# Loading the input of a last-axis product in two chunks

## The chip, the cores and the metric

The kernel runs on one core of a Trainium2 chip. The metric is the device time of one execution in microseconds (us). The trace of an execution covers less than that: its span is 8.4 us where the device time is 10.19 us.

Three engines matter here: SyncE (SP) issues the transfers, 16 DMA engines carry them out in pieces called packets, and VectorE (DVE) multiplies. For the load of the kernel before, the trace shows 128 data packets, 16 semaphore packets (9 ns each) and 16 semaphore records, from 3.42 to 3.99 us. Here a transfer counts as landed at the last of its 16 records; the first multiply starts 0.023 us after it.

Runs are labelled fast or slow. For a program on one core the label only says whether a run is within 1.5% of the fastest run of the same kernel in its session. One execution in each set is profiled.

## The reference

```python
batch, seq, dim = 32, 64, 64
x = np.random.randn(batch, seq, dim).astype(np.float32) * 0.1 + 1.0
np.prod(x, axis=-1)          # 2048 products of 64 numbers each
```

The input is 512 KB of fp32, the output 8 KB.

## The kernel before

The 2048 rows are laid out as 128 partitions with 16 rows each, so that a partition holds 16 x 64 = 1024 elements, 4 KB. One load brings all of it. A tree of six multiplies then halves the rows: 512 products per partition, then 256, 128, 64, 32 and 16.

```python
x_view = xf.rearrange("(p n) d -> p n d", p=P)       # P = 128, n = 16
out_view = of.rearrange("(p n) -> p n", p=P)
with tc.tile_pool(name="sbuf", bufs=1) as pool:
    xt = pool.tile([P, n, R], x.dtype, name="xt")    # R = 64
    nc.sync.dma_start(out=xt[:], in_=x_view)
    cur = xt; cur_len = R; lvl = 0
    while cur_len > 1:
        half = cur_len // 2
        nxt = pool.tile([P, n, half], x.dtype, name=f"lvl{lvl}")
        nc.vector.tensor_tensor(out=nxt[:], in0=cur[:, :, 0:half],
                                in1=cur[:, :, half : 2 * half], op=mult)
        # ... (a branch for odd lengths, not taken here)
        cur = nxt; cur_len = half; lvl += 1
    nc.sync.dma_start(out=out_view, in_=cur[:, :, 0])
```

## Time and profile before

| | us |
|---|---|
| median of 6 runs | 10.19 (10.13 to 10.23) |
| span of the trace | 8.4 |
| load: issue to landing | 0.72 to 3.99 |
| six multiplies: first start to issue of the store | 4.01 to 6.21 |
| store: issue to landing | 1.4 |

The chain of work that ended last, in order of time (start in us, length in us, what; "issue" lines cut). It is one line with no branches: load, then multiplies.

```profile
0.72 3.26 DMA xt<-in_x_dram
...
4.01 0.70 DVE lvl_60 L51
...
4.73 0.43 DVE lvl_62 L51
...
6.00 0.17 DVE lvl_70 L51
```

The groups of instructions of the same kernel: line, engine, operation, output and input, shapes, count, then busy us and mean ns of one, then the idle time before it and what ended it. VectorE (DVE) is idle for 4.0 us and is released by the load. Halving the elements does not halve the time: 691 ns at 512 elements, 424 at 256, 174 at 16.

```profile
L51 DVE TENSOR_TENSOR lvl_60<-xt 128x512 f32<-128x512 f32 x1 | 0.7, 691 | 4.0 <-DMA xt<-in_x_dram 4.0
L51 DVE TENSOR_TENSOR lvl_62<-lvl_60 128x256 f32<-128x256 f32 x1 | 0.4, 424 | 0.0
L51 DVE TENSOR_TENSOR lvl_64<-lvl_62 128x128 f32<-128x128 f32 x1 | 0.3, 291 | 0.0
L51 DVE TENSOR_TENSOR lvl_66<-lvl_64 128x64 f32<-128x64 f32 x1 | 0.2, 226 | 0.0
L51 DVE TENSOR_TENSOR lvl_68<-lvl_66 128x32 f32<-128x32 f32 x1 | 0.2, 193 | 0.0
L51 DVE TENSOR_TENSOR lvl_70<-lvl_68 128x16 f32<-128x16 f32 x1 | 0.2, 174 | 0.0
```

The DMA row of the page shows the span in 40 slices of 0.21 us, in GB/s. Data flow from the ninth slice, 1.0 us after the issue at 0.72 us, and start slower than they go on: 195 to 254 GB/s in the first three slices, up to 429 later.

```profile
GB/s 0 0 0 0 0 0 0 0 195 254 215 390 312 371 429 254 78 0 0 0 0 0 0 0 0 0 0 0 0 0 0 0 0 22 17 0 0 0 0 0
```

The packet records behind that row: 128 packets of 4 KB, which is eight for each of 16 engines, from 1.72 to 3.64 us, typically 159 ns each. The semaphores that report the landing come in between 3.42 and 3.99 us.

### The profile page before, as it was taken

The numbers are of one execution on the slowest core, as the hardware profiler recorded it, in microseconds if no ns is written. First come the engines' busy times: TensorE is split into PE (matmuls) and PEld (weight loads), VectorE is DVE, ScalarE is ACT, GpSimd is POOL, SyncE is SP. The second block draws the span as 40 slices with busy tenths as digits, with TensorE's granted clock in tenths as the row PEclk, the third lists the DMA queues.
The fourth block names the chain that finished last, engine by engine and source line by source line (L and its number), as shares of the span: only waits on it lengthen the run. The fifth ranks groups of instructions, "written<-read, shape, count | busy, mean of one in ns | idle before, by whom it ended". The sixth has DMA issues, their size and how long they took to land.

```text
span 8.4 us, 50 instructions
## 1 busy us (share of the span) xinstructions
DVE 2.0 (24%) x6; POOL 0.2 (2%) x4
## 2 busy tenths in 40 slices
DVE  0000000000000000000999898988840000000000
POOL 0900000000000000000000000000000000000000
DMA  0000000089797996200000000000000002200000
GB/s 0 0 0 0 0 0 0 0 195 254 215 390 312 371 429 254 78 0 0 0 0 0 0 0 0 0 0 0 0 0 0 0 0 22 17 0 0 0 0 0
DMA packets 289, 0.53 MB, mean 63 GB/s; under 512 B 161, under 2 KB 161, under 8 KB 289
## 3 DMA queue, kind: packets, MB, share of 16 engines
q1 hardware_dynamic: 288, 0.53, 19.8%
q14 instruction: 1, 0.00, 0.0%
HBM read 0.52 MB, written 0.01 MB: 63 GB/s over the span
## 4 chain that ended last, share of the span: by engine, by line
DMA 39%; DVE 24%; issue 2%
DMA xt<-in_x_dram 39%; DVE lvl_60 L51 8%; DVE lvl_62 L51 5%; DVE lvl_64 L51 4%; DVE lvl_66 L51 3%; DVE lvl_68 L51 2%; DVE lvl_70 L51 2%
## 5 line engine op out<-in xcount | busy, mean ns | idle before, releaser
L51 DVE TENSOR_TENSOR lvl_60<-xt 128x512 f32<-128x512 f32 x1 | 0.7, 691 | 4.0 <-DMA xt<-in_x_dram 4.0
L51 DVE TENSOR_TENSOR lvl_62<-lvl_60 128x256 f32<-128x256 f32 x1 | 0.4, 424 | 0.0
L51 DVE TENSOR_TENSOR lvl_64<-lvl_62 128x128 f32<-128x128 f32 x1 | 0.3, 291 | 0.0
L51 DVE TENSOR_TENSOR lvl_66<-lvl_64 128x64 f32<-128x64 f32 x1 | 0.2, 226 | 0.0
L51 DVE TENSOR_TENSOR lvl_68<-lvl_66 128x32 f32<-128x32 f32 x1 | 0.2, 193 | 0.0
L51 DVE TENSOR_TENSOR lvl_70<-lvl_68 128x16 f32<-128x16 f32 x1 | 0.2, 174 | 0.0
L85 POOL MEMSET const-float32-0.0<- 128x1 f32 x1 | 0.1, 98 | 0.2 <-issue 0.2
L85 POOL MEMSET const-bfloat16-1.0<- 128x1 bf16 x1 | 0.1, 101 | 0.0
L85 POOL MEMSET const-uint8-127<- 128x1 uint8 x1 | 0.1, 101 | 0.0
L85 POOL MEMSET const-float32-1.0<- 128x1 f32 x1 | 0.1, 98 | 0.0
## 6 DMA issues: line engine op xcount, KB each, us to landing
xt<-in_x_dram SPq DMA_DIRECT2D x1, 512.0 KB, 3.3
out_dram<-lvl_70 SPq DMA_DIRECT2D x1, 8.0 KB, 1.4
```

Source lines behind the costliest of these rows:

```text
L51: nc.vector.tensor_tensor(out=nxt[:], in0=cur[:, :, 0:half], in1=cur[:, :, half : 2 * half], op=mybir.AluOpType.mult,)
L85: nc = _bacc.Bacc("TRN2", target_bir_lowering=False, num_devices=1)
```

## The change

The intent is to load the input in two chunks of 8 rows per partition, and to do the first two levels of the tree on chunk 0 while chunk 1 is still on its way. Both chunks write into one tile `comb`, from which the last four levels run unsplit. The diff also adds branches for other shapes and axes, which this input does not take; they are cut here.

```diff
-        xt = pool.tile([P, n, R], x.dtype, name="xt")
-        nc.sync.dma_start(out=xt[:], in_=x_view)
-        ... six multiplies over all 16 rows
+NSPLIT = 2
+PER_CHUNK_LEVELS = 2
...
+                comb = pool.tile([P, nr, w_comb], x.dtype, name="comb", tag="comb")
+                for k in range(nsplit):
+                    kr0 = r0 + k * cr
+                    comb_k = comb[:, k * cr : (k + 1) * cr, :]
+                    xt = pool.tile([P, cr, R], x.dtype, name=f"xt{k}", tag=f"xt{k}")
+                    nc.sync.dma_start(out=xt[:], in_=x_view[:, kr0 : kr0 + cr, :])
...
+                    for lv in range(per_chunk_levels):
...
+                        _level(nc, cur, dst)       # dst is comb_k in the last of them
...
+                res = _prod_tree(nc, pool, comb[:], x.dtype, tag="lvl")
+                nc.sync.dma_start(out=out_view[:, r0:r1], in_=res[:, :, 0])
```

The multiplies become `c0l` and `comb` of chunk 0 (256 and 128 elements per partition), the same for chunk 1 (`c1l`, `comb`), and then 128, 64, 32 and 16 elements.

## The prediction

> **What bounds the kernel now.** The chain of waits is one serial line. The load of 512 KB is issued at 0.72 us and lands at 3.99 us (3.26 us, 39% of the 8.4 us span); only then does VectorE start (timeline: first multiply at 4.01 us, after 4.0 us idle). The six multiplies take 691, 424, 291, 226, 193 and 174 ns (groups of instructions), with about 34 ns between starts and ends, so the store is issued at 6.21 us. The store takes 1.4 us to land (DMA issues); then comes a closing part, and 1.8 us lie outside the span (10.19 against 8.4).
>
> The load itself: the packets in the trace start at about 1.72 to 2.04 us, 1.0 us after the issue, staggered over the 16 engines by about the length of the issuing instruction (367 ns). After slow first packets (up to 466 ns) an engine takes 159 ns per 4 KB packet, eight packets each; the last data packet ends at 3.60 us, the last semaphore at 3.99 us.
>
> **What the change does.** Two chunks of 8 rows per partition. One load becomes two of 256 KB from the same queue, with 2 KB runs instead of 4 KB. Levels 1 and 2 are done per chunk, (512, 256) elements becoming 2 x (256, 128); the other four multiplies are unchanged, as is the store. VectorE's total rises from 2.00 us to 2.00 - 691 - 424 + 2 x (424 + 291) ns = 2.31 us. [...]
>
> **Critical path.** The second issue starts about 0.40 us after the first, near 1.12 us; [...] chunk 0's eight half-size packets (estimate: 80 ns each plus the slow start, 0.9 us) keep each engine busy to about 2.6 to 2.9 us. So the stream should not pause, and chunk 0 lands near 3.1 us. Its two multiplies (424 + 291 + gaps, 0.78 us) end near 3.9 us, before chunk 1 lands. After chunk 1's landing remain 424 + 291 + 291 + 226 + 193 + 174 = 1599 ns instead of 1999: 0.40 us saved. Given back: twice as many packets. [...] with an extra semaphore packet (9 ns in the trace) per engine I estimate 0.03 to 0.1 us, so chunk 1 lands near 4.05 us. One more semaphore to wait for or clear in the closing part: 0 to 0.06 us.
>
> **Prediction.** 10.19 - 0.40 + 0.06 + 0.03 = 9.88 us, 3% faster; 8 in 10 between 9.74 and 10.04. Faster by over 2%: 0.76; within 2%: 0.21; slower by over 2%: 0.03.
>
> **What would show each step.** Two issues about 0.40 us apart; first load landing at 2.9 to 3.3 us, second at 3.95 to 4.2; VectorE idle between chunk 0's second multiply and chunk 1's first one, ended by the second load; from the last landing to the store's issue 1.80 us instead of 2.20; packets of 2 KB near 80 ns; the store at 1.4 us.
>
> **What would make it wrong.** The second load starting its data only about 1 us after the first's last descriptor[...]: chunk 1 lands at 4.2 us or later and the gain halves. Chunk 0 landing late, its slowest engine waiting behind chunk 1's packets, so that its multiplies hold chunk 1 up. A longer closing part from the added semaphore.

## The result, and the profile after

The changed kernel took 9.97 us (median of 10 runs, 9.89 to 10.18) against 10.22 us for the kernel before (20 runs, 10.13 to 10.29). The ratio is 0.973 with a 95% interval of 0.968 to 0.978. Ratios here are the mean time of one kernel's fast runs over that of the other's of the same rounds, so they are not quite the ratio of the medians.

Two things make this result less firm than its interval. The ten runs fall in two groups, 9.89 to 10.00 us and 10.07 to 10.18 us, and the second group is what the label calls slow and leaves out. With all ten counted, the ratio of the means is 10.01 / 10.22 = 0.980. And the same kernel was measured three times more, on three chips:

| run | chip | before, us | changed, us | ratio of fast runs | 95% interval |
|---|---|---|---|---|---|
| first result | not recorded | 10.22 | 9.97 | 0.973 | 0.968 to 0.978 |
| e1_after_again | 4 | 10.20 | 10.11 | 0.991 | 0.987 to 0.995 |
| e8_after_again2 | 13 | 10.15 | 9.82 | 0.966 | 0.961 to 0.970 |
| e9_after_again3 | 7 | 10.20 | 10.01 | 0.971 | 0.961 to 0.980 |

The medians of the kernel before stay within 0.07 us of each other; those of the changed kernel range over 0.29 us. The gain is clear of noise in each session but lies between 0.9% and 3.4%. The ratio of e9 rests on two of its six runs; with all six it is 0.981.

The first profile after fell in a slow run (10.27 us). These are lines of its chain; chunk 0 landed at 3.81 us, and chunk 0's load and multiplies are on the chain.

```profile
0.73 3.08 DMA xt_59<-in_x_dram
...
3.83 0.44 DVE c0l_61 L24
...
4.29 0.29 DVE comb L24
4.58 0.34 DVE c1l_66 L24
```

Two profiles of fast runs of the same kernel were taken later, e1 (10.13 us) and e8 (9.83 us), and they show two different limits. First e8, its timeline (start, length, engine, line, operation, output and input; in brackets the idle time before it and what ended it; where two loads are meant, x2):

```profile
0.73 0.85 SPq L134 DMA_DIRECT2D xt<-in_x_dram  x2
3.40 0.42 DVE L24 TENSOR_TENSOR c0l<-xt 128x256 f32<-128x256 f32 x1 [3.40 <-DMA xt<-in_x_dram]
3.86 0.29 DVE L24 TENSOR_TENSOR comb<-c0l 128x128 f32<-128x128 f32 x1
4.07 0.42 DVE L24 TENSOR_TENSOR c1l<-xt 128x256 f32<-128x256 f32 x1
4.52 0.29 DVE L24 TENSOR_TENSOR comb<-c1l 128x128 f32<-128x128 f32 x1
...
5.86 0.35 SPq L158 DMA_DIRECT2D out_dram<-lvll  x1
```

There is no idle time before `c1l`: VectorE never waits again after its first multiply. The chain of e8 says the same, as it runs through chunk 0's load and both its multiplies:

```profile
0.73 2.65 DMA xt<-in_x_dram
...
3.40 0.43 DVE c0l L24
...
3.86 0.29 DVE comb L24
4.15 0.35 DVE c1l L24
```

Now the same lines of e1, first the timeline, then the chain. VectorE is idle for 0.19 us before `c1l`, and the chain goes through the second load, issued at 1.16 us and landed at 4.34 us.

```profile
3.42 0.42 DVE L24 TENSOR_TENSOR c0l<-xt 128x256 f32<-128x256 f32 x1 [3.42 <-DMA xt<-in_x_dram]
3.88 0.29 DVE L24 TENSOR_TENSOR comb<-c0l 128x128 f32<-128x128 f32 x1
4.36 0.43 DVE L24 TENSOR_TENSOR c1l<-xt 128x256 f32<-128x256 f32 x1 [0.19 <-DMA xt<-in_x_dram]
...
6.16 0.35 SPq L158 DMA_DIRECT2D out_dram<-lvll  x1
```

```profile
1.11 0.05 issue
1.16 3.18 DMA xt<-in_x_dram
4.34 0.02 issue
4.36 0.44 DVE c1l L24
```

With the landings from the semaphore records of the traces, the change of time can be added up. All three are fast runs:

| us | before | e8 | e1 |
|---|---|---|---|
| chunk 0 lands | | 3.381 | 3.392 |
| last chunk lands | 3.986 | 3.983 | 4.336 |
| its first multiply starts | 4.009 | 4.071 | 4.359 |
| store issued | 6.207 | 5.858 | 6.155 |
| end of span less issue of store | 2.189 | 2.190 | 2.195 |
| store issued earlier than before by | | 0.349 | 0.052 |
| run time less than before's 10.19 by | | 0.36 | 0.06 |

In each kernel an undelayed first multiply starts 0.023 us after the landing. From there to the store the kernel before takes 6.207 - 4.009 = 2.198 us, e8 5.858 - 4.071 = 1.787 us and e1 1.796 us. So the shorter chain saves 0.41 us in e8 and 0.40 us in e1. In e8 nothing is lost at the landing (-0.003 us), but `c1l` starts 4.071 - 3.983 - 0.023 = 0.065 us late because VectorE is still at chunk 0. In e1 the landing is 0.350 us late and the hold-up is zero. The closing part did not change.

Three more profiles have the same loads and the same order of multiplies: the first one after and e9, both labelled slow, and e10, fast, with other addresses for its chunks. They show both losses at once. In them chunk 1 landed 0.58 to 0.61 us after chunk 0, as in e8 (0.60; in e1 it was 0.94), and `c1l` was held up by 0.087, 0.083 and 0.064 us; the last landing was 0.41, 0.10 and 0.13 us later than before's. One caution: the landing of a single load moves too. It came at 4.07 us in e12 and at 4.12 us in e2 (both labelled slow), so a difference of 0.1 us between two profiles is not yet the effect of the split.

The windows view shows the two late stretches of the load in these runs (stretch, us, DVE busy, POOL busy, clock, DMA share, GB/s). Before, then e8, then e1:

```profile
3.20:3.60 0.40, 0.00 (x0) 0.00 (x0) 1.00 0.34 133
3.60:4.00 0.40, 0.00 (x0) 0.00 (x0) 1.00 0.00 0
```

```profile
3.20:3.60 0.40, 0.20 (x1) 0.00 (x0) 1.00 0.38 138
3.60:4.00 0.40, 0.37 (x2) 0.00 (x0) 1.00 0.01 5
```

```profile
3.20:3.60 0.40, 0.18 (x1) 0.00 (x0) 1.00 0.39 143
3.60:4.00 0.40, 0.36 (x2) 0.00 (x0) 1.00 0.09 36
```

A DMA share of 0.09 of 16 engines is one to two engines. In e1 nearly all of the data have come by 3.6 us, as in the others, and one or two engines are still at work to 4.02 us. The landing, at 4.336 us, comes after the end of that work. By the packet records, the last seven packets of e1 follow each other from 3.46 to 4.02 us and take 81 to 84 ns each: they started late, they were not slow.

### The profile page after: what moved, and what is told of

It reads as the page before. It is cut to its first block, busy times and chain, and to the rows that moved or that the text cites. A ratio compares the mean times of both kernels' runs of the same rounds, so it can differ in the third digit from the quotient of the medians.

```text
span 8.5 us, 54 instructions
## 1 busy us (share of the span) xinstructions
DVE 2.2 (26%) x8; POOL 0.2 (2%) x4
## 4 chain that ended last, share of the span: by engine, by line
DMA 36%; DVE 27%; issue 3%
DMA xt_59<-in_x_dram 36%; DVE comb L24 7%; DVE c0l_61 L24 5%; DVE c1l_66 L24 4%; DVE lvll_69 L24 4%; DVE lvll_71 L24 3%; DVE lvll_73 L24 2%; DVE lvll_75 L24 2%
## 5 line engine op out<-in xcount | busy, mean ns | idle before, releaser
L24 DVE TENSOR_TENSOR comb<-c0l_61 128x128 f32<-128x128 f32 x1 | 0.3, 293 | 0.0
L24 DVE TENSOR_TENSOR comb<-c1l_66 128x128 f32<-128x128 f32 x1 | 0.3, 293 | 0.0
```

Source lines behind the costliest of these rows:

```text
L24: nc.vector.tensor_tensor(out=dst[:, :, 0:half], in0=src[:, :, 0:half], in1=src[:, :, half : 2 * half], op=MULT,)
```

## The experiments

Two theories stood against each other after the result. Theory S is the prediction: chunk 0's work is hidden, and the time hangs on chunk 1's landing. Theory H: chunk 0 lands so late that its multiplies hold chunk 1 up. Later runs ask why chunk 1 lands late at all. Twelve runs were made, of ten kernels (e1, e8 and e9 are the changed one), each in five rounds; all results were correct except where a wrong result was intended.

### e1: the changed kernel again

No edit.

> The changed kernel unaltered, to get a profile of a fast run (the first one fell in a slow run) and a second measure of the ratio. Theory H (hold-up): chunk 0 lands so late that its two multiplies (0.78 us with gaps) end after chunk 1 has landed; VectorE then never idles after its first multiply and the chain is chunk 0's landing + 2.46 us; chunk 0 lands at 3.4 to 3.6 us, chunk 1 at 3.95 to 4.2 us. Rival S (stream, as predicted): chunk 0 lands at 2.9 to 3.3 us, VectorE idles 0.1 us or more before chunk 1's first multiply, and the store is issued 1.80 us after chunk 1's landing. Both: ratio 0.965 to 0.98.

Measured: 10.11 us, ratio 0.991, outside the expected 0.965 to 0.98. The profile, shown above, is a mixture. VectorE idles, and the store follows chunk 1's landing by 1.82 us, as S has it. But chunk 0 landed at 3.39 us, just past the 2.9 to 3.3 us of S, and chunk 1 at 4.34 us, past both theories. Here the load's end is the limit.

### e2: one load, multiplies in chunks

```diff
-level over xt[:, 0:16]; level over the result
+for a, b in [(0, 8), (8, 16)]:
+    level(nc, half[:], xt[:, a:b, :])
+    level(nc, comb[:, a:b, :], half[:])
```

> One 512 KB load as before, but the multiplies as in the change (levels 1 and 2 in two chunks of rows). Measures the added VectorE work alone: 2.46 us from first multiply to store issue instead of 2.20, so before + 0.26 us (10.48, ratio 1.025). Both theories expect the same; if it is under 1.015 my costing of the small multiplies is wrong.

Measured: 10.27 us, ratio 1.0025 (0.998 to 1.007): my costing was wrong by its own rule. The build had put both 256-element multiplies ahead of both 128-element ones. The timeline shows why they cost so little. Two multiplies of 422 ns on average take 0.76 us together, and the first of the next pair starts at 4.83 us, before the pair ends at 4.91 us.

```profile
4.15 0.76 DVE L15 TENSOR_TENSOR c<-xt 128x256 f32<-128x256 f32 x2 [4.15 <-DMA xt<-in_x_dram]
4.83 0.49 DVE L15 TENSOR_TENSOR comb<-c 128x128 f32<-128x128 f32 x2
5.35 0.29 DVE L15 TENSOR_TENSOR t<-comb 128x128 f32<-128x128 f32 x1
```

A multiply that does not need the result of the one in front starts 342 ns after it (4.149 and 4.491 us) instead of the 458 ns (3.404 and 3.862 us in e8) of a multiply that waits for a 256-element one. First multiply to store is 6.365 - 4.149 = 2.216 us, against 2.198 us before. (This profile is of a slow run; these durations agree with those of fast runs.) The changed kernel has the order chunk 0, chunk 0, chunk 1, chunk 1, and so has one such overlap, `c1l` over `comb`: 4.071 - 3.862 = 209 ns after it, where a waiting one needs 325. Its first multiply to store is 2.454 us.

So in both profiles a multiply that waits for no result starts some 0.12 us earlier than one that waits: 458 - 342 = 116 ns in e2, 325 - 209 = 116 ns in e8.

### e3: two loads, multiplies uncut

```diff
-nc.sync.dma_start(out=xt[:], in_=x_view)
+for a, b in [(0, 8), (8, 16)]:
+    nc.sync.dma_start(out=xt[:, a:b, :], in_=x_view[:, a:b, :])
```

> Two 256 KB loads, then the six whole multiplies of before. Measures what splitting the load costs at the last landing, closing part included. Theory S, as predicted: 0.06 to 0.15 us (10.28 to 10.37, ratio 1.006 to 1.015), last landing near 4.05. Theory H needs no particular value. Over 0.25 us would say that the second load does not follow the first without a pause.

Measured: 10.52 us (10.42 to 10.55), ratio 1.029. The profiled run, at 10.42 the fastest of them, adds up: the last landing at 4.148 us is 0.162 us later than before, and the first multiply follows it by 0.101 us instead of 0.023; it waits for two loads. (In e5, also with two loads, it follows the landing by 5.50 - 5.40 = 0.10 us, in e6, with one, by 4.50 - 4.48 = 0.02 us.) Together 0.24 us, which is how much later the store is issued. Four of the other five runs were 0.09 us or more slower still, which no profile shows. So on this chip a second load seems to cost some 0.16 us or more at the landing, not the 0.06 us of the prediction. This compares one profile with before's, which was taken in other runs than e3's; that the runs of e3 are 0.32 us slower than before's in the same rounds, of which the extra wait explains 0.08 us, points the same way.

### e4: chunk 0's multiplies taken out

```diff
+nc.vector.memset(comb[:, 0:8, :], 1.0)     # wrong result on purpose
 for k, (a, b) in enumerate([(0, 8), (8, 16)]):
     ... load chunk k
+    if k == 0: continue
```

> The change with chunk 0's two multiplies taken out (its half of comb is set to 1.0 before the data comes; both loads stay; wrong result on purpose). Theory H: chunk 0's multiplies held chunk 1 up, so this is faster than the changed kernel by 0.1 to 0.25 us (9.7 to 9.8, ratio to before 0.95 to 0.96). Rival S: they were hidden, so same time as the changed kernel within 0.03 us (ratio 0.97 to 0.975).

Measured: 10.00 us, ratio 0.978, against 10.11 us and 0.991 of e1 on the same chip. The sign is H's, and S's "same within 0.03 us" failed. But the size, 0.11 us between the medians, is more than the hold-up that any profile shows (0.06 to 0.09 us in four, none in e1). The e4 profile fell in a slow run and can't be compared with e1's. The run does not decide between less hold-up and an earlier landing.

### e5: two loads by partition halves

```diff
-nc.sync.dma_start(out=xt[:], in_=x_view)
+for a, b in [(0, 64), (64, 128)]:
+    nc.sync.dma_start(out=xt[a:b], in_=x_view[a:b])
```

> Two loads, each of 64 partitions with the 4 KB runs of before, then the six whole multiplies. e3 (two loads of 2 KB runs) cost 0.30 us, of which about 0.07 us is the extra semaphore wait on VectorE. Theory P (packet size: small packets make the last landing late): here only the extra wait and closing part remain, ratio 1.00 to 1.012. Rival D (a second load instruction makes it late, whatever the packets): as e3, ratio 1.022 to 1.035.

Measured: 11.66 us (11.44 to 11.72; five of six above 1.5% of the fastest, so no ratio was formed) against 10.15: a miss for both theories, and no test of them. The 4 KB packets took 265 ns in the median instead of 159, and the last landing came at 5.40 us. Why the packets took longer is not shown. The data also started late, 1.33 us after the first issue.

### e6: one load of 2 KB runs

```diff
-xt = pool.tile([P, n, R], ...)
+xt = pool.tile([P, 2, 9, R], ...)          # a gap after each 8 rows
-nc.sync.dma_start(out=xt[:], in_=x_view)
+nc.sync.dma_start(out=xt[:, :, 0:8, :], in_=xf.rearrange("(p k m) d -> p k m d", p=P, k=2))
```

> One load instruction with 256 runs of 2 KB (the tile has a gap between its halves), then the six whole multiplies; no second semaphore. Theory P: about e3 without the extra wait, ratio 1.015 to 1.028. Rival D: ratio 0.998 to 1.008, since only the 16 x 80 ns against 8 x 155 ns per engine (0.04 us) are added.

Measured: 10.61 us, ratio 1.046, beyond both theories. The issue of the load takes 0.62 us, where the load of before took 0.37, and the data flow only from the tenth slice of 0.22 us. The timeline's load and the page's row:

```profile
0.73 0.62 SPq L60 DMA_DIRECT2D xt<-in_x_dram  x1
```

```profile
GB/s 0 0 0 0 0 0 0 0 0 83 83 138 359 396 405 359 423 102 9 0 0 0 0 0 0 0 0 0 0 0 0 0 0 2 35 0 0 0 0 0
```

The packet records start at 2.12 us instead of 1.72 and end at 4.13 us: 2.01 us of data instead of 1.92. In this profile the landing (4.479 us) is 0.49 us later than before's: 0.40 us is the later start, and 0.09 us the longer stretch of data. The smaller packets can explain most of the latter (16 x 84 against 8 x 159 ns per engine is 0.07 us). Why the start is late is not shown: this load has twice as many runs, but in e5 loads with half as many started 1.33 us after the issue, and in e10 a load with 128 runs started after 1.26 us. In e8 and e1 the first data come at 1.72 and 1.74 us, so the change did not pay this there.

### e7 and e10: chunks that are contiguous in memory

e3's chunk takes every other 2 KB of x. In e7 and e10 each chunk is one contiguous 256 KB piece. Rows then come in another order. e7 is e3 with this edit, e10 the changed kernel with it. Their outputs are wrong, which doesn't matter for the times.

```diff
+xc = xf.rearrange("(c p m) d -> c p m d", c=2, p=P)
-    ... in_=x_view[:, a:b, :]
+    ... in_=xc[k]
```

> As e3, but each load reads one contiguous 256 KB piece of x instead of every other 2 KB (rows come in another order, wrong result on purpose). Theory A (the access pattern in memory, every other 2 KB, slows the first packets): ratio 1.005 to 1.015. Theories P and D: as e3, ratio 1.022 to 1.035.

Measured: 10.31 us, ratio 1.015, at the edge of theory A. But e7 ran on chip 13 and e3 on chip 4, and on chip 13 the changed kernel itself did far better. So it was repeated in the form of e10 with a control on the same chip.

> The changed kernel with each chunk one contiguous 256 KB piece of x (rows in another order, wrong result on purpose; loads, multiplies and store otherwise the same). Theory A (every other 2 KB of memory makes chunk 1 land late): faster than e9 by 0.05 us or more where e9 lands late, ratio 0.955 to 0.97, chunk 1 landing at 4.05 us or before. Rival N (the delay is chance of the engines' start, whatever the pattern): same as e9 within 0.03 us of its mean; e7's better ratio than e3's was then the chip.

Measured: 9.96 us, ratio 0.980, beside e9 with 10.01 us and 0.971. The means of all six runs are 9.963 and 9.995 us, within the 0.03 us or so that rival N gave. Theory A's forecast failed: the ratio was to be 0.955 to 0.97 and its interval is 0.975 to 0.985. No effect of the pattern is seen, but the six runs of e9 scatter too much (the 95% interval of the difference is some 0.13 us either way) to rule out the 0.05 us that A asked for. The runs with contiguous chunks scatter less, 0.12 us in e10 against 0.31 us in e9, which may be chance in six runs each. The profile of e10 is again of the held-up kind: landings at 3.512 and 4.118 us, `c1l` at 4.205, 0.064 us after it could have started.

### e8 and e9: the changed kernel twice more

> The changed kernel once more, to see how repeatable its gain is: ratios of 0.973 and 0.991 were measured in two sessions. If the difference is the session's chip or placement, runs here cluster at one level within 0.1 us; if it is chance from run to run, both levels (9.9 and 10.15 us) appear here as they did in the first session. VectorE's chain after chunk 1's landing is 1.80 us in the profile in either case.

> The changed kernel again, as the control for e10 on the same chip. So far 0.973 (two levels in one session), 0.991 with chunk 1 landing at 4.34 us, and 0.966 with chunk 1 landing at 3.98 us. If the gain is 0.40 us minus the delay of chunk 1's landing against before (3.99 us), the store is issued 1.80 us after that landing, or, where chunk 1 lands less than 0.75 us after chunk 0, some 0.05 us later.

Measured: 9.82 us and ratio 0.966 on chip 13, 10.01 us and 0.971 on chip 7. On chip 13 the six runs cluster within 0.11 us. On chip 7 they spread over both levels (9.80 to 10.11 us; four of six are labelled slow). The profile of e9 (9.95 us, labelled slow) has its landings at 3.494 and 4.082 us and the hold-up of 0.083 us that the expectation allowed for. So both the chip or session and chance from run to run have a part. The profile of e8 and its sum are in the section before: 0.065 us of hold-up and no landing delay. What makes single engines finish late is left open.

### e11 and e12: a reduction instead of the tree

Chunks of 8 rows in e11; e12 is the same with one load of all 16 rows.

```diff
-... eight multiplies
+    nc.vector.tensor_reduce(out=res[:, a:b], in_=xt[:], axis=mybir.AxisListType.X, op=MULT)
```

> A version meant to beat both: the two loads, and one product-reduction instruction for each chunk instead of eight multiplies. If a reduction of 512 elements takes what a 512-element multiply does (0.69 us, an estimate from the trace), 0.72 us remain after chunk 1's landing instead of 1.80: about 1.08 us faster than e9, 8.75 to 9.05 us, ratio 0.86 to 0.89.

> One load and one product-reduction of 1024 elements [...]: 0.95 us faster than before, 9.2 to 9.3 us, ratio 0.905 to 0.915. The difference to e11 is what the split is worth once the compute is short: 0.53 us of reduction hidden less the landing delay.

Measured: e11 8.97 us, ratio 0.874 (0.866 to 0.883); e12 9.29 us, ratio 0.904 (0.898 to 0.911); both times as expected, e12's ratio by a hair under its range. The reduction of e12 can be estimated from the trace of before: 691 ns at 512 elements and 424 at 256 are 267 ns for 256 elements more, so 691 + 2 x 267 = 1225 ns at 1024, if a reduction follows the multiplies' slope; it took 1219. The groups of instructions, e11 first, then e12:

```profile
L63 DVE TENSOR_REDUCE res<-xt 128x8 f32<-128x512 f32 x2 | 1.3, 686 | 3.6 <-DMA xt<-in_x_dram 3.6
```

```profile
L63 DVE TENSOR_REDUCE res<-xt 128x16 f32<-128x1024 f32 x1 | 1.2, 1219 | 4.1 <-DMA xt<-in_x_dram 4.1
```

One reduction of 1024 elements takes 1.22 us where the six multiplies take 2.00, and it has no gaps in between. A reduction of 512 takes what a multiply with 512 results does, 686 against 691 ns, but it reads 512 elements and finishes them. In this form the split is worth 9.29 - 8.97 = 0.32 us. e11 beats both kernels.

## Why the prediction was right or wrong

The predicted time, 9.88 us within 9.74 to 10.04, held for the first result (9.97 us; 3.0% predicted, 2.7% measured by the ratio of fast runs, 2.0% with all ten). It would have failed on chip 4 (10.11 us). Point by point:

- **The chain to be shortened: right.** Of the chain from chunk 1's first multiply to the store, 0.40 us was to be saved; 0.41 us (e8) and 0.40 us (e1) were.
- **Issues, packets, closing part: right.** The second load is issued 0.43 us after the first (predicted 0.40) and 2 KB packets take 84 ns (predicted 80), which is 0.07 us more per engine than the 4 KB packets and agrees with the author's estimate of 0.03 to 0.1 us. The closing part grew by 0.001 to 0.006 us (predicted 0.03, at most 0.06, an estimate of the author's).
- **"Chunk 0 lands near 3.1 us": wrong, and with it the idle VectorE.** It landed at 3.38 and 3.39 us in the two fast profiles. The prediction's own numbers said so. If the stream does not pause, chunk 1 follows chunk 0 by its own eight packets, 8 x 80 = 0.64 us, and a landing of chunk 1 at 4.05 us puts chunk 0 at 3.4. The semaphores' 0.35 us after the last packet, readable in the trace of before, was also not added in full to the 2.9 us at which chunk 0's packets were to end. The landings lay 0.60 us apart in e8, while VectorE is free for chunk 1 only 4.071 - 3.404 = 0.667 us after it starts on chunk 0. Hence the hold-up of 0.065 us (0.06 to 0.09 us in four of five profiles), named in the prediction as a way to fail and not counted.
- **VectorE's added work: wrong in size, without harm.** The prediction has chunk 0's two multiplies block VectorE for 0.78 us. It was 0.667 us, because the next, independent multiply starts before the last one ends (4.071 us against 3.862 + 0.291 = 4.153 us in e8). With 0.78 us the hold-up would have been 0.18 us.
- **"Chunk 1 lands near 4.05 us": a term of the sum mis-sized.** Predicted was a delay of 0.03 to 0.1 us; the trace of before shows 9 ns of it, the extra semaphore packet, and the rest was the author's estimate. Measured were none in e8, 0.16 us in e3 and 0.35 us in e1. The counted cause, more packets, is small: e6 shows 0.09 us more data time. In e1 the rest is one or two engines that finish late, at 4.02 us. Contiguous chunks did not change the mean measurably (e10). Why an engine is late is not settled, nor whether it belongs to the chip or to where a session's buffers lie.

So the mechanism was right, but the near hit in size is in part luck. In e8 the 0.065 us of hold-up, not counted, took the place of 0.06 us for the landing and 0.03 us for the closing part, counted and not found. In e1 the hold-up was absent and the landing 0.35 us late. Which of these mixtures the fast runs of the first result had is not shown, as none of them was profiled. The two losses trade places from run to run, so a single profile does not give their shares.

## What to carry to other kernels

When one transfer is split in two without a pause, expect the second chunk to land after the first by about its own streaming time (here 0.58 to 0.61 us in four profiles of five, for eight packets of 84 ns or 0.67 us; 0.94 us in e1, where an engine was late); compare that with the work on the first chunk before counting it as hidden, and add the delay from the last packet to the semaphore (0.35 us before, 4.336 - 4.02 = 0.32 us in e1) to both. A gain of 0.4 us out of 10 hung here on the engines that finished last (in e1 one or two of 16 worked to 4.02 us, and the landing was 0.35 us late), so measure it in several sessions before trusting an interval from one. And look first at the work that remains after the last landing: replacing the tree by one reduction was worth 10.20 - 9.29 = 0.91 us, the split 0.09 to 0.33 us.
